# A fixed order on TensorE in the modulation loop, x loaded between weights, and one projection less ahead of a scan tree

## The chip, the cores and the metric

The kernel runs on one core of one Trainium2 chip. The metric is the device time of one execution in microseconds (us). Three timed executions of the kernel before gave 2169.12, 2169.86 and 2171.75 us. The changed kernel is timed in the same way.

The engines are named as the profile names them: PE is TensorE (matmuls), PEld its weight loads, DVE is VectorE, ACT is ScalarE, POOL is GpSimd, and SP is SyncE, which here only issues DMA transfers. Every engine works through its own list of instructions strictly in order; a waiting instruction holds up all that stand behind it.

## The reference

The reference is one layer of a hybrid network on 1024 latent tokens of width 1024, with 256 context tokens beside them. All data is fp32. What matters here is its beginning:

```python
m_lat = (jax.nn.silu(c) @ w_mod[l] + b_mod[l]).reshape(B_, 1, N_MOD, D)
m_ctx = (jax.nn.silu(c_ctx) @ w_mod[l] + b_mod[l]).reshape(N_MOD, D)
h_lat = rms_norm(x, norm_mix[l]) * (1.0 + m_lat[:, :, 1]) + m_lat[:, :, 0]
h_ctx = rms_norm(ctx, norm_mix[l]) * (1.0 + m_ctx[1]) + m_ctx[0]
... = features(h_lat, w_in[l], ...)        # one projection for three mixers and the gates
... = features(h_ctx, w_in[l], ...)
yc_ctx, s_f, s_b = hgrn2_bidir(ccq, ccf, ccb, cci, ccg, lbf[l], lbb[l], gn_c[l], s0, s0)
yc = hgrn2_bidir(cq, cf, cb, ci, cg, lbf[l], lbb[l], gn_c[l], s_f, s_b)[0]
```

So the modulation vectors come first, then the normed and modulated context and latents, then the projections of the context. A gated recurrence over the context gives a state per head and direction (`s_f`, `s_b`), and the same recurrence over the latents starts from it. Its forget gates use lower bounds `lbf`, `lbb`, which depend on two small inputs alone. Windowed and global attention, the merge of the branches and a gated MLP follow. The change leaves all of them as they are.

## The kernel before, in words

Tiles have 128 partitions; the width 1024 is cut into `KT` = 8 blocks. A large matmul is done in three products (high part by high part, high by low, low by high), for which ACT casts a weight tile to its high part (`w_unit`, L174) and DVE subtracts to get the low part (L175). The raw weights go through three rotating buffers each of the tags `wr`, `wh` and `wl`; the context's weights are used raw (`w_raw`, L186).

A scheduling layer sets the order of instructions on each engine. It takes the program's operations, their dependences, their place in the program and priorities (`tc.high_priority`), and decides which ready operation comes next on each engine; a pool hands out the buffers. The order is fixed when the program is built.

The stages that the change touches, in order of time:

- **The modulation loop** (L312 to L350). Eight weight tiles `wm0` to `wm7` of 1 MB are loaded by SP. For six of them PE multiplies by `silu(c)` (`pr`, L331), ACT copies the row out (L333), PE turns it (`pm`, L293) and DVE makes shift and scale of it (L284, L286). For blocks 1 and 4 (`MOD_OFF`) DVE does the product itself (`acc`, L322 and L325), and PE only turns the result (`pt`, L344). At `i == NORMAT` (3) `ctx_norm` makes the context's RMS: ACT squares, DVE sums (`css`, L300), PE turns (`rcc`, L237), DVE and POOL take the power -1/2 (L247, L248), and PE spreads the result over all partitions with two matmuls (`rpc`, L258). From then on `ctx_h` makes the modulated context block by block: DVE L306, ACT L308 (`ch`). The tiles `pr`, `pt` and `rpc` share two PSUM banks of tag "b".
- **The lower bounds** (L351 to L360): a load of 4 KB, six small DVE operations and one exponential on ACT, after the loop.
- **The context's projections, woven with the latents' norm** (`weave` at L458). `ctx_c` does for four heads the units f, b and v (`czf`, `czb`, `czv`), `ctx_kv` then keys and values (`ckv`). `lat_norm` loads x row-wise (`xn`, four buffers), squares and sums it on ACT (L380), then loads x turned, as eight tiles of 512 KB (`x32`, L384), spreads the RMS (`rpx`), and makes from each tile the high and low parts `hh` and `hl` of the normed latents with two DVE operations and one on ACT (`finish_h`, L263 to L265).
- **The early projections**: `zq` and `zf` of head 0 (48 matmuls of 512 columns each). Only two tiles of this kind (`mm2`) fit at once, so the third, `zb`, waits until `zq` has been read by ACT (L1037) and DVE (`qr`, L1038).
- **The context's recurrence.** DVE folds the keys in a tree of eight levels (L473, L476); for each head PE turns the result (`ckp`, L483), ACT copies it (`ckt`, L485), PE multiplies it with the values (`cu`, L489) and ACT copies the state out (`st_ctx`, L490). `ckt` has one buffer.
- **The recurrence over the latents** (`hgrn_head`), attention, merge and MLP, some 2000 us, follow.

Of the kernel before, what the change touches and what calls it, by code (L numbers as in the profile page):

```python
# [12 lines left out]
AF = mybir.ActivationFunctionType  # L13
ALU = mybir.AluOpType
# [4 lines left out]
P = 128  # L19
D = 1024  # L20
KT = D // P
L = 1024
LT = L // P
LC = 256
# [22 lines left out]
WAT = 5  # L47
MPRIO = 100
CXAT = 1
NORMAT = 3  # L50

MOD_OFF = (1, 4)
# [38 lines left out]
def build(tc, ins, out, dbg=None):  # L91
    nc = tc.nc
    V, A, G, T, SP = nc.vector, nc.scalar, nc.gpsimd, nc.tensor, nc.sync
    with ExitStack() as top:
# [46 lines left out]
        lbr = cs([P, 8], "lbr")  # L141
# [60 lines left out]
        def gemm_tm(psl, ws, h, toks, k0=0, nk=KT):  # L202

            hh, hl = h
            for k in range(nk):
# [3 lines left out]
                T.matmul(psl, hh[:, k, toks], wl[:, k % 4, :], start=False, stop=False)  # L209
                T.matmul(psl, hl[:, k, toks], wh[:, k % 4, :], start=False, stop=e)  # L210


        def rms_row(pool, parts, n, name, tag="b", on_pe=False):

            return rms_bc(rms_r(pool, parts, n, name, on_pe), n, name, tag)
# [45 lines left out]
        def finish_h(t, r, a, bi, ohh, ohl, x=None):  # L261

            V.scalar_tensor_tensor(out=t, in0=t if x is None else x, scalar=a, in1=r, op0=ALU.mult, op1=ALU.mult)  # L263
            A.activation(ohh, t, AF.Identity, bias=bi)
            V.scalar_tensor_tensor(out=ohl, in0=t, scalar=bi, in1=ohh.bitcast(F32), op0=ALU.add, op1=ALU.subtract)  # L265

        with ExitStack() as s0:
# [28 lines left out]
            def ctx_norm():  # L296
                csq = xm_.tile([P, KT, LC], F32, tag="csq", name="csq")
                A.activation(csq, cx, AF.Square)
                css = xm_.tile([P, LC], F32, tag="css", name="css")
                V.reduce_sum(out=css, in_=csq.rearrange("p k t -> p t k"), axis=AX.X)  # L300
                return rms_row(xm_, [css], LC, "c")

            def ctx_h():
                while pend:
# [2 lines left out]
                                           op0=ALU.mult, op1=ALU.mult)  # L307
                    A.activation(ch[:, k], cx[:, k], AF.Identity, bias=m01[:, k, 0, 1:2])  # L308

            for i in range(KT):  # L310
                wm = xm_.tile([P, 2, KT, P], F32, tag="wm", name=f"wm{i}", bufs=WM)
                SP.dma_start(wm, ins["w_mod01"][i].rearrange("p (j k c) -> p j k c", j=2, k=KT))  # L312
                if i == CXAT:
                    SP.dma_start(cx, ins["ctxT"].rearrange("(k p) t -> p k t", p=P))
                if WAT <= i < WAT + 3:
                    units0.append(w_raw(ins["w_cm"][U_C["fbv"[i - WAT]]], KT, P))
                if i in MOD_OFF:
                    acc = accs[i] = xm_.tile([P, 2, 2, P], F32, tag="acc", name=f"acc{i}", bufs=2)
                    for k in range(KT):
                        for v in range(2):  # L320
                            if k == 0:
                                V.tensor_scalar(out=acc[:, v], in0=wm[:, :, k], scalar1=scc[:, k, v:v + 1], scalar2=None,  # L322
                                                op0=ALU.mult)
                            else:
                                V.scalar_tensor_tensor(out=acc[:, v], in0=wm[:, :, k], scalar=scc[:, k, v:v + 1],  # L325
                                                       in1=acc[:, v], op0=ALU.mult, op1=ALU.add)
                    continue
                pr = bank("b", f"pr{i}", (P, 2, P))
                with tc.high_priority(offset=MPRIO):
                    for k in range(KT):  # L330
                        T.matmul(pr[0:2], scc[:, k], wm[:, :, k], start=k == 0, stop=k == KT - 1)  # L331
                    row = xm_.tile([2, 2, P], F32, tag="row", name=f"row{i}", bufs=3)
                    A.copy(row, pr[0:2])  # L333
                rows.append((i, row))
                if len(rows) > 1:
                    mod_row(*rows.pop(0))
                if i == KT - 1:
                    mod_row(*rows.pop(0))
                for n in MOD_FIN.get(i, ()):
                    pm = xm_.tile([P, 2, 2], F32, tag="pm", name=f"pm{n}")  # L340
                    pt = bank("b", f"pt{n}", (P, 2, 2, P))
                    for v in range(2):
                        for j in range(2):
                            T.transpose(pt[:, j, v], accs[n][:, v, j], ident)  # L344
                    V.reduce_sum(out=pm, in_=pt, axis=AX.X)
                    mod_done(n, pm)
                if i == NORMAT:
                    rc = ctx_norm()
                if i >= NORMAT:
                    ctx_h()  # L350
            SP.dma_start(lbr, ins["lb"])  # L351
            SP.dma_start(gnc, ins["gn"])

            V.tensor_tensor(out=lt, in0=lbr, in1=lbr, op=ALU.subtract)
            A.activation(lt, lt, AF.Exp)
            V.reciprocal(lb, lt)
            V.tensor_tensor(out=lt, in0=lt, in1=lb, op=ALU.mult)
            V.tensor_tensor(out=lt, in0=lt, in1=lt, op=ALU.subtract)
            V.tensor_scalar(out=lb, in0=lt, scalar1=0.0, scalar2=1.0, op0=ALU.max, op1=ALU.min)
            V.tensor_scalar(out=oml, in0=lb, scalar1=-1.0, scalar2=1.0, op0=ALU.mult, op1=ALU.add)  # L360
            xw.close()
            hpool = top.enter_context(ExitStack())
            hp = Aligned(hpool.enter_context(tc.tile_pool(name="hp", bufs=1, reuse_waits="tile")))
# [8 lines left out]
            def lat_norm():  # L372

                nt = L // P
                rl = xq.tile([P, nt], F32, tag="rs", name="rsx")
                for t in range(nt):
                    xn = xq.tile([P, D], F32, tag="xn", name=f"xn{t}", bufs=4)
                    SP.dma_start(xn, ins["x"][t * P:(t + 1) * P, :])
                    sq = xq.tile([P, D], F32, tag="sq", name=f"sqx{t}", bufs=2)
                    A.activation(sq, xn, AF.Square, accum_out=rl[:, t:t + 1])  # L380
                    if t % 2:
                        yield
                for k in range(KT):
                    SP.dma_start(x32[:, k], ins["xT"][k * P:(k + 1) * P, :])  # L384
                rp = rms_bc(rms_pow(rl), L, "x", "b")
                yield
                for k in range(KT):
                    finish_h(x32[:, k], rp, a01[:, k, 0:1], m01[:, k, 0, 0:1], hh[:, k], hl[:, k])
                    yield

            def proj(nm, h):

                w = w_unit(ins["w_cm"][U_C[nm] + h], KT, P)
                z = mm2(f"z{nm}{h}")
                for hf in range(2):
                    gemm_cm(z[:, hf], w, H, slice(hf * 512, hf * 512 + 512))
                return z.rearrange("p a b -> p (a b)")
# [1 line left out]

            knb = ct([P, 64], "knb")  # L400
            qnb = ct([P, 64], "qnb")
            A.dma_start(knb, ins["kn"].to_broadcast([P, 64]))
            A.dma_start(qnb, ins["qn"].to_broadcast([P, 64]))
            cp = Aligned(s0.enter_context(tc.tile_pool(name="cp", bufs=1, reuse_waits="tile")))
            cK = cp.tile([P, 2, CH, LC], F32, tag="cK", name="cK")
            cF = cp.tile([P, 2, CH, LC], F32, tag="cF", name="cF")
# [24 lines left out]

            def ctx_kv():

                for br in range(2):
                    ws = [w_raw(ins["w_tm"][(br * 3 + 2) * 2 + kh], 4, 256) for kh in range(2)]
                    for tt in range(2):
                        z = bank("b", f"ckv{br}{tt}", (P, 256))
                        for k in range(KT):
                            T.matmul(z, ch[:, k, tt * P:(tt + 1) * P], ws[k // 4][:, k % 4], start=k == 0,
                                     stop=k == KT - 1)  # L440
                        kv = cp.tile([P, 256], F32, tag="ckvs", name=f"ckvs{br}{tt}", bufs=2)
                        if br == 0:
# [15 lines left out]
            weave((ctx_all(), 14), (lat_norm(), 13))  # L458
            xin.close()

            early = {(nm, 0): proj(nm, 0) for nm in "qf"}
            cp2 = Aligned(s0.enter_context(tc.tile_pool(name="cp2", bufs=1, reuse_waits="tile")))

            Fp = cF
# [1072 lines left out]
```

## Time and profile before

| | us |
|---|---|
| three timed executions, lowest / median / highest | 2169.12 / 2169.86 / 2171.75 |
| the profiled execution's own time | 2173.9 |
| its span from first to last instruction | 2172.1 |
| PE busy | 2092.8 |
| DVE, ACT, POOL busy | 1434.3, 993.6, 396.1 |
| DMA, HBM read and written | 181.68 MB and 45.61 MB |

The profile is one execution, recorded by the hardware. A row of the timeline gives the start, the duration, the engine, the line, the operation and its tiles, and in brackets how long the engine sat idle just before and what ended that. The view of waits sums such idle time by what ended it. A table of windows gives for chosen stretches each engine's busy time, the clock that TensorE was granted (1.00 is full speed), the share of the DMA engines that was busy, and GB/s. A row of a group has the number of instructions behind the x, then busy us and mean ns. Durations of matmuls overlap: one record of 0.39 us follows another after 0.23 us.

### The profile page before, as it was taken

The numbers are of one execution on the slowest core, as the hardware profiler recorded it, in microseconds if no ns is written. First come the engines' busy times: TensorE is split into PE (matmuls) and PEld (weight loads), VectorE is DVE, ScalarE is ACT, GpSimd is POOL, SyncE is SP. The second block draws the span as 40 slices with busy tenths as digits, with TensorE's granted clock in tenths as the row PEclk, the third lists the DMA queues.
The fourth block names the chain that finished last, engine by engine and source line by source line (L and its number), as shares of the span: only waits on it lengthen the run. The fifth ranks groups of instructions, "written<-read, shape, count | busy, mean of one in ns | idle before, by whom it ended". The sixth has DMA issues, their size and how long they took to land. (4 is left out here: it accounts for less than half of the span.)

```text
span 2172.1 us, 30936 instructions
## 1 busy us (share of the span) xinstructions
PE 2092.8 (96%) x11610; PEld 1737.9 (80%) x11610; DVE 1434.3 (66%) x2578; ACT 993.6 (46%) x1800; POOL 396.1 (18%) x374
## 2 busy tenths in 40 slices
PE   7999999999999999999999999999899999999997
PEld 3878888789988788877777788887788888888887
DVE  4736666636566677679999856668877777764433
ACT  3323333311122777677777743445444444453322
POOL 0000000001022122123323300011434433200111
PEclk9999999999999999999999999999999999999999
DMA  8511110126653211221010254551222222286342
GB/s 323 219 46 31 49 46 29 53 82 195 197 163 116 92 54 45 71 66 30 30 35 27 69 198 159 179 169 61 93 77 84 87 79 88 79 276 199 106 129 91
DMA packets 95493, 229.30 MB, mean 106 GB/s; under 512 B 10736, under 2 KB 35824, under 8 KB 94320
## 3 DMA queue, kind: packets, MB, share of 16 engines
q1 hardware_dynamic: 95056, 227.26, 31.6%
q8 instruction: 91, 1.49, 0.3%
q14 instruction: 58, 0.48, 0.1%
q10 hardware_dynamic: 288, 0.07, 0.0%
HBM read 181.68 MB, written 45.61 MB: 105 GB/s over the span
## 5 line engine op out<-in xcount | busy, mean ns | idle before, releaser
L175 DVE TENSOR_TENSOR wl<-wr,wh 128x1024 fp32r<-128x1024 f32 x137 | 173.0, 1264 | 246.3 <-ACT wh L174 233.0
L174 ACT CAST wh<-wr 128x1024 fp32r<-128x1024 f32 x137 | 142.9, 1044 | 411.0 <-PE dn L903 71.7
L1279 DVE TENSOR_TENSOR pl<-pp,ph 128x512 fp32r<-128x512 f32 x236 | 159.0, 684 | 9.8 <-ACT ph L1278 8.5
L198 PE MATMUL gz<-hh,wh 128*128 128x512 f32 x384 | 156.3, 407 | 4.1 <-ACT gs L508 4.0
L1278 ACT CAST ph<-pp 128x512 fp32r<-128x512 f32 x236 | 136.3, 585 | 43.7 <-PE pp L1274 40.2
L200 PE MATMUL gz<-hh,wl 128*128 128x512 f32 x384 | 151.7, 395 | 0.0
L199 PE MATMUL gz<-hl,wh 128*128 128x512 f32 x384 | 151.6, 395 | 0.0
L209 PE MATMUL tm<-wl,hh 128*128 128x256 f32 x384 | 108.9, 284 | 2.7 <-DVE wl L175 2.7
L208 PE MATMUL tm<-wh,hh 128*128 128x256 f32 x384 | 108.8, 283 | 0.1
L210 PE MATMUL tm<-wh,hl 128*128 128x256 f32 x384 | 108.7, 283 | 0.0
L1269 PE MATMUL po<-pl,VHL 128*128 128x512 f32 x236 | 98.9, 419 | 7.6 <-DVE pl L1279 7.3
L1268 PE MATMUL po<-ph,VHL 128*128 128x512 f32 x236 | 104.8, 444 | 1.3 <-ACT ph L1278 1.3
L903 PE MATMUL dn<-ac,wh 128*128 128x512 f32 x256 | 99.7, 390 | 0.0
L904 PE MATMUL dn<-ac,wl 128*128 128x512 f32 x256 | 99.6, 389 | 0.0
L902 PE MATMUL dn<-ac,wh 128*128 128x512 f32 x256 | 99.6, 390 | 0.0
L1274 PEld LDWEIGHTS pp<-ident,plat 128*128 128x128 f32 x512 | 61.2, 140 | 34.3 <-DVE pl L1279 21.8
L1274 PE MATMUL pp<-ident,plat 128*128 128x128 f32 x512 | 78.2, 275 | 10.2 <-DVE pl L1279 9.9
L198 PEld LDWEIGHTS gz<-hh,wh 128*128 128x128 f32 x384 | 72.7, 189 | 18.4 <-ACT gs L508 6.2
L200 PEld LDWEIGHTS gz<-hh,wl 128*128 128x128 f32 x384 | 72.5, 189 | 15.3
L199 PEld LDWEIGHTS gz<-hl,wh 128*128 128x128 f32 x384 | 72.7, 189 | 11.6
L716 ACT ACTIVATE u<-c,cw 128x1024 f32<-128x1024 f32 x40 | 49.8, 1246 | 68.1 <-DVE c L863 37.1
L209 PEld LDWEIGHTS tm<-wl,hh 128*128 128x128 f32 x384 | 73.7, 192 | 3.7 <-DVE wl L175 3.4
(1478 smaller groups left out, 6094.5 us busy)
## 6 DMA issues: line engine op xcount, KB each, us to landing
wr<-in_w_cm SPq DMA_DIRECT2D x48, 512.0 KB, 3.7
wr<-in_w_up SPq DMA_DIRECT2D x44, 512.0 KB, 3.5
wr<-in_w_down SPq DMA_DIRECT2D x33, 512.0 KB, 3.7
wmr<-in_w_mod SPq DMA_DIRECT2D x32, 512.0 KB, 4.4
gate_d<-gs SPq DMA_DIRECT2D x48, 256.0 KB, 2.3
sgt<-gate_d SPq DMA_DIRECT2D x24, 512.0 KB, 3.3
act_d<-u SPq DMA_DIRECT2D x22, 512.0 KB, 2.6
st<-act_d SPq DMA_DIRECT2D x44, 256.0 KB, 4.5
```

The costliest lines, as they stand in the source:

```text
L174: A.copy(hi[:, :n], raw[:, :n])
L175: (lo_eng or V).tensor_tensor(out=lo[:, :n], in0=raw[:, :n], in1=hi[:, :n].bitcast(F32), op=ALU.subtract)
L198: T.matmul(psl, wh[:, k, c], hh[:, k0 + k, cols], start=s, stop=False)
L199: T.matmul(psl, wh[:, k, c], hl[:, k0 + k, cols], start=False, stop=False)
L200: T.matmul(psl, wl[:, k, c], hh[:, k0 + k, cols], start=False, stop=e)
L208: T.matmul(psl, hh[:, k, toks], wh[:, k % 4, :], start=s, stop=False)
L209: T.matmul(psl, hh[:, k, toks], wl[:, k % 4, :], start=False, stop=False)
L210: T.matmul(psl, hl[:, k, toks], wh[:, k % 4, :], start=False, stop=e)
L1268: T.matmul(po, vv, ph, start=n == 0, stop=False)
L1274: T.transpose(pp[:, h], PT(h, n), ident)
L1278: A.copy(ph, pp)
L1279: V.tensor_tensor(out=pl, in0=pp, in1=ph.bitcast(F32), op=ALU.subtract)
```

## The change

Five edits, all in the first part of the program:

1. The modulation loop is put into a section in which PE's instructions keep the order in which the code writes them. For that the code spreads the context's RMS (`rms_bc`, the matmuls `rpc`) at `i == NORMAT + 2` and no longer right after the norm, and `ctx_h` runs from there.
2. The lower bounds move from behind the loop into it, at `i == LBAT` (3).
3. Four of the eight tiles of turned x are loaded before the RMS is spread, and the other four one by one, each with a step of `finish_h`, so that they stand between the context's weights in SP's list.
4. Three small loads (`knb`, `qnb` from ACT's list, `gnc` from behind the loop) move into `ctx_kv` on SP.
5. Only `zq` is written ahead of the tree. `zf` comes from `hgrn_head`, so behind the tree and `cu` in the program.

```diff
+LBAT = 3
...
+        def lower_bounds():
+
+            SP.dma_start(lbr, ins["lb"])
+            V.tensor_tensor(out=lt, in0=lbr, in1=lbr, op=ALU.subtract)
+            A.activation(lt, lt, AF.Exp)
...
-                return rms_row(xm_, [css], LC, "c")
+                return rms_r(xm_, [css], LC, "c", False)
...
+            mo = ExitStack()
+            mo.enter_context(tc.manual_schedule(engines={mybir.EngineType.PE}))
             for i in range(KT):
...
+                if i == LBAT:
+                    lower_bounds()
...
                 if i == NORMAT:
                     rc = ctx_norm()
-                if i >= NORMAT:
+                if i == NORMAT + 2:
+                    rc = rms_bc(rc, LC, "c", "b")
+                if i >= NORMAT + 2:
                     ctx_h()
-            SP.dma_start(lbr, ins["lb"])
-            SP.dma_start(gnc, ins["gn"])
...
+            mo.close()
...
-                for k in range(KT):
-                    SP.dma_start(x32[:, k], ins["xT"][k * P:(k + 1) * P, :])
+                def x_load(k):
+                    if k < KT:
+                        SP.dma_start(x32[:, k], ins["xT"][k * P:(k + 1) * P, :])
+
+                for k in range(4):
+                    x_load(k)
                 rp = rms_bc(rms_pow(rl), L, "x", "b")
                 yield
                 for k in range(KT):
+                    x_load(k + 4)
                     finish_h(x32[:, k], rp, a01[:, k, 0:1], m01[:, k, 0, 0:1], hh[:, k], hl[:, k])
...
-            A.dma_start(knb, ins["kn"].to_broadcast([P, 64]))
-            A.dma_start(qnb, ins["qn"].to_broadcast([P, 64]))
...
+                SP.dma_start(knb, ins["kn"].to_broadcast([P, 64]))
+                SP.dma_start(qnb, ins["qn"].to_broadcast([P, 64]))
+                SP.dma_start(gnc, ins["gn"])
...
-            early = {(nm, 0): proj(nm, 0) for nm in "qf"}
+            early = {("q", 0): proj("q", 0)}
```

How this moves instructions is seen at three places. The first is PE's list in the modulation loop, from the turn of the context's sums (`rcc0`) to the first context unit (`czf0`). Before:

```order
L237 MATMUL rcc0_203<-ident_89,css_200 128x128 x2
L293 MATMUL pm3_252<-ident_89,row3_182 128x2 x2
L258 MATMUL rpc_209<-ident_89,rsc_202 128x128
L331 MATMUL pr5_241<-wm5_237,scc_83 2x256 x8
L258 MATMUL rpc_209<-ident_89,rsc_202 128x128
L293 MATMUL pm5_274<-ident_89,row5_250 128x2 x2
L331 MATMUL pr6_263<-wm6_259,scc_83 2x256 x8
L344 MATMUL pt4_280<-ident_89,acc4_220 128x128 x4
L293 MATMUL pm6_307<-ident_89,row6_272 128x2 x2
L331 MATMUL pr7_296<-wm7_292,scc_83 2x256 x8
L293 MATMUL pm7_312<-ident_89,row7_305 128x2 x2
L420 MATMUL czf0_350<-ch_111,wr1_239 128x256 x8
```

And the same place now:

```order
L249 MATMUL rcc0_213<-ident_89,css_210 128x128 x2
L347 MATMUL pr5_242<-wm5_238,scc_83 2x256 x8
L305 MATMUL pm3_253<-ident_89,row3_192 128x2 x2
L270 MATMUL rpc_258<-ident_89,rsc_212 128x128 x2
L347 MATMUL pr6_273<-wm6_269,scc_83 2x256 x8
L305 MATMUL pm5_284<-ident_89,row5_251 128x2 x2
L360 MATMUL pt4_290<-ident_89,acc4_221 128x128 x4
L347 MATMUL pr7_306<-wm7_302,scc_83 2x256 x8
L305 MATMUL pm6_317<-ident_89,row6_282 128x2 x2
L305 MATMUL pm7_322<-ident_89,row7_315 128x2 x2
L432 MATMUL czf0_350<-ch_111,wr1_240 128x256 x8
```

The product `pr5` has moved ahead of the two matmuls `rpc`, between which it stood, and `pm6` has moved behind `pr7`.

The second place is SP's list where the turned x (`x32`) is loaded; `wr7`, `wh8`, `wl9` are the context's weights f, b, v of the third head, and the next three those of the fourth. Before:

```order
L186 DMA wl6_480<-in_w_cm 128x1024
L384 DMA x32_116<-in_xT 128x1024 x8
L186 DMA wr7_503<-in_w_cm 128x1024
L186 DMA wh8_522<-in_w_cm 128x1024
L186 DMA wl9_541<-in_w_cm 128x1024
L186 DMA wr10_564<-in_w_cm 128x1024
```

Now:

```order
L394 DMA x32_116<-in_xT 128x1024 x4
L187 DMA wr7_500<-in_w_cm 128x1024
L187 DMA wh8_520<-in_w_cm 128x1024
L394 DMA x32_116<-in_xT 128x1024
L187 DMA wl9_540<-in_w_cm 128x1024
L394 DMA x32_116<-in_xT 128x1024
L187 DMA wr10_564<-in_w_cm 128x1024
L394 DMA x32_116<-in_xT 128x1024
```

Four loads of x, not eight, now stand ahead of `wr7`; the rest alternate with the weights.

The third place is PE's list around the context's recurrence, between the early projections and `zb`. Before, behind all 48 matmuls of `zf0`:

```order
L200 MATMUL zf0_762<-hh_334,wl18_759 128x512
L483 MATMUL ckp0_844<-ident_89,cK_347 128x128 x4
L483 MATMUL ckp1_859<-ident_89,cK_347 128x128 x4
L489 MATMUL cu00_851<-cV_349,ckt0_849 128x128 x2
L489 MATMUL cu01_855<-cV_349,ckt0_849 128x128 x2
L483 MATMUL ckp2_874<-ident_89,cK_347 128x128 x4
L489 MATMUL cu10_866<-cV_349,ckt1_864 128x128 x2
L489 MATMUL cu11_870<-cV_349,ckt1_864 128x128 x2
L483 MATMUL ckp3_889<-ident_89,cK_347 128x128 x4
```

Now, behind all of `zq0`:

```order
L201 MATMUL zq0_710<-hh_336,wl17_707 128x512
L498 MATMUL ckp0_792<-ident_89,cK_347 128x128 x4
L498 MATMUL ckp1_807<-ident_89,cK_347 128x128 x4
L199 MATMUL zf0_872<-hh_336,wh18_868 128x512
L200 MATMUL zf0_872<-hl_337,wh18_868 128x512
L504 MATMUL cu00_799<-cV_349,ckt0_797 128x128 x2
L504 MATMUL cu01_803<-cV_349,ckt0_797 128x128 x2
L498 MATMUL ckp2_822<-ident_89,cK_347 128x128 x4
L201 MATMUL zf0_872<-hh_336,wl18_869 128x512
L199 MATMUL zf0_872<-hh_336,wh18_868 128x512
L504 MATMUL cu10_814<-cV_349,ckt1_812 128x128 x2
L504 MATMUL cu11_818<-cV_349,ckt1_812 128x128 x2
```

The recurrence's small matmuls have moved from behind `zf0` into its beginning, two to four matmuls of `zf0` between one head's and the next. Behind `zb0` PE's list is the same as before.

More of the change, by code (lines that the diff above doesn't have):

```diff
@@ L210, in gemm_tm @@
                 T.matmul(psl, hl[:, k, toks], wh[:, k % 4, :], start=False, stop=e)
+        def lower_bounds():
+            SP.dma_start(lbr, ins["lb"])
+            V.tensor_tensor(out=lt, in0=lbr, in1=lbr, op=ALU.subtract)
+            A.activation(lt, lt, AF.Exp)
+            V.reciprocal(lb, lt)
+            V.tensor_tensor(out=lt, in0=lt, in1=lb, op=ALU.mult)
+            V.tensor_tensor(out=lt, in0=lt, in1=lt, op=ALU.subtract)
+            V.tensor_scalar(out=lb, in0=lt, scalar1=0.0, scalar2=1.0, op0=ALU.max, op1=ALU.min)
+            V.tensor_scalar(out=oml, in0=lb, scalar1=-1.0, scalar2=1.0, op0=ALU.mult, op1=ALU.add)
         def rms_row(pool, parts, n, name, tag="b", on_pe=False):
@@ L348, in build @@
                     rc = ctx_norm()
-                if i >= NORMAT:
+                if i == NORMAT + 2:
+                    rc = rms_bc(rc, LC, "c", "b")
+                if i >= NORMAT + 2:
                     ctx_h()
-            SP.dma_start(lbr, ins["lb"])
-            SP.dma_start(gnc, ins["gn"])
[L354 to L360, printed above, removed]
+            mo.close()
             xw.close()
```

## The prediction

> **What bounds the kernel now.** I read the page's first lines, then a table of four stages, then PE's waits in the first three of them, then the places where these waits stand.
>
> ```profile
> span 2172.1 us, 30936 instructions
> PE 2092.8 (96%) x11610; PEld 1737.9 (80%) x11610; DVE 1434.3 (66%) x2578; ACT 993.6 (46%) x1800; POOL 396.1 (18%) x374
> ...
> core 0: us, PE busy (x) PEld busy (x) DVE busy (x) ACT busy (x) POOL busy (x), PEclk, DMA share, GB/s
> 0.00:42.96 42.96, 29.08 (x120) 11.12 (x121) 23.06 (x67) 11.50 (x22) 1.36 (x6) 0.96 0.86 334
> 42.96:103.94 60.98, 58.43 (x330) 52.83 (x329) 40.99 (x62) 28.33 (x50) 2.54 (x2) 0.97 0.64 237
> 103.94:150.76 46.82, 42.11 (x195) 34.57 (x193) 10.43 (x16) 9.68 (x21) 0.87 (x2) 0.93 0.18 55
> 150.76:2172.10 2021.34, 1963.15 (x10971) 1639.39 (x10969) 1359.79 (x2433) 944.12 (x1709) 391.29 (x365) 1.00 0.30 98
> ```
>
> PE is busy 96% of the span, and from 150.76 us on, where its order is unchanged, 97% at full clock. So what PE gains before 150.76 should move all the rest forward, and the question is how much it gains in three stages: the modulation loop (to 42.96), the context's projections (to 103.94), and `zq`, `zf`, the context's recurrence and `zb` (to 150.76). PE's waits there:
>
> ```profile
> PE pr L331 <- DMA wm<-in_w_mod: 8.8, 2, 7.7
> PE czf L420 <- DMA wr<-in_w_cm: 2.6, 1, 2.6
> PE zb L198 <- DVE qr L1038: 2.5, 1, 2.5
> PE rpc L258 <- POOL rsc L248: 2.3, 1, 2.3
> PE cu L489 <- ACT ckt L485: 2.2, 4, 0.8
> ```
>
> The 8.8 us are the first loads, which the change doesn't touch. Behind three of the others (`czf`, `zb`, `rpc`) the clock drops, which costs nearly as much again:
>
> ```profile
> 25.00:30.00 5.00, 3.74 (x10) 1.25 (x11) 4.58 (x14) 0.00 (x0) 0.88 (x1) 0.66 1.01 413
> ...
> 65.07:67.60 2.53, 0.00 (x0) 0.02 (x1) 2.53 (x3) 1.44 (x3) 0.00 (x0) 1.00 1.02 409
> 67.60:72.80 5.20, 5.18 (x16) 4.35 (x17) 5.20 (x6) 2.59 (x3) 0.00 (x0) 0.67 1.03 410
> ...
> 125.80:137.20 11.40, 6.69 (x51) 5.50 (x49) 2.96 (x5) 7.36 (x16) 0.00 (x0) 0.94 0.22 65
> 137.20:142.49 5.29, 5.29 (x13) 4.13 (x14) 3.06 (x3) 0.52 (x1) 0.00 (x0) 0.50 0.00 0
> ...
> 150.76:161.64 10.88, 10.88 (x50) 9.01 (x48) 9.62 (x14) 4.00 (x6) 0.00 (x0) 1.00 0.15 48
> ```
>
> **Part A, the modulation loop.** The timeline of PE:
>
> ```profile
> 23.40 0.38 PE L237 MATMUL rcc<-ident,css 128*128 128x128 f32 x2
> ...
> 26.26 0.32 PE L258 MATMUL rpc<-ident,rsc 128*128 128x128 f32 x1 [2.27 <-POOL rsc L248]
> ...
> 26.51 5.30 PE L331 MATMUL pr<-wm,scc 128*2 128x256 f32 x16
> ...
> 31.74 0.32 PE L258 MATMUL rpc<-ident,rsc 128*128 128x128 f32 x1
> ...
> 32.53 3.62 PE L331 MATMUL pr<-wm,scc 128*2 128x256 f32 x16
> ...
> 38.09 3.62 PE L331 MATMUL pr<-wm,scc 128*2 128x256 f32 x16 [0.57 <-DVE pm L345]
> ...
> 42.75 0.28 PE L293 MATMUL pm<-ident,row 2*128 2x2 f32 x2 [1.04 <-ACT row L333]
> 42.96 3.72 PE L420 MATMUL czf<-ch,wr 128*128 128x256 f32 x16
> ```
>
> PE waits 2.27 us for POOL with the first `rpc`, while `pr5` stands behind it; then the second `rpc` stands behind `pr5`, so DVE's first product with it starts only at 32.1. Now `pr5` fills the wait. From the end of `rcc` (23.8, or 24.1, since `pm0` now stands behind `pr2` and takes its 0.3 here) I add: `pr5` 3.45 at full clock to 27.55; `pm3` 0.3; `rpc`, whose input comes at about 28.0 as DVE has 1.5 us of lower bounds ahead of it, to 28.4; `pr6` 3.45; `pm5` 0.3; then, as in the rows between 32.53 and 42.96, a wait of 0.5, `pt4` 0.66, a wait of 0.6, `pr7` 3.45, `pm6` 0.28, a wait of 0.5 and `pm7` 0.28. That ends at 38.5 in place of 42.96. The weights don't set it:
>
> ```profile
> 13.19 0.33 SPq L312 DMA_DIRECT2D wm<-in_w_mod  x1
> ...
> DMA to landing us min/median/max: 5.0/13.8/18.1
> ```
>
> That is the last issue of `wm7`, and the longest time to landing of all eight: it is there by 31.3, and `pr7` starts at 34.0 in my sum. The unknown is the lower bounds. DVE now waits for their load in the middle of the loop, and the norm's sums stand behind it.
>
> ```profile
> lbr<-in_lb SPq DMA_DIRECT2D x1, 4.0 KB, 14.0
> ```
>
> Issued at about 6 us, right behind `wm3`, it lands between 18 (`wm3`'s landing, as transfers end nearly in their order here) and 20; DVE is busy with the context's sum to 20.0. So 0 to 1 us is lost, and ACT's exponential may hold up a row by 0.5. I take 4.2 us for A, between 2 and 5.
>
> **Part B, the context's projections.** PE stands still for 2.53 us at 65.07 because `wr7` is late, and then does `czf` in 5.20 us at a clock of 0.67, where a unit otherwise follows after 3.45. That is 2.53 + 1.75 = 4.3 us. Why it is late:
>
> ```profile
> 42.47 6.41 SPq L378 DMA_DIRECT2D xn<-in_x  x4
> ...
> 49.41 4.60 SPq L384 DMA_DIRECT2D x<-in_xT  x8
> 55.74 0.33 SPq L186 DMA_DIRECT2D wr<-in_w_cm  x1
> 57.01 0.33 SPq L186 DMA_DIRECT2D wh<-in_w_cm  x1
> ```
>
> It stands behind eight loads of 512 KB. At 410 GB/s one takes 1.28 us, which is also the distance of the last two issues. Four fewer ahead bring it 5.1 us earlier, at about 62.5. But PE also asks earlier, by the 4.2 us of A. What feeds the x loads comes earlier too: SP issued the fifth `xn` at 42.47 only when ACT had squared the first, behind the modulation's rows, and ACT now gets there some 3 to 4 us sooner. So `wr7` lands at about 59 and is needed at 61.8. The loads behind it alternate, 2.56 us for a weight and an x, against 3.45 of PE for a unit. The last x tiles come later, and DVE makes `hl` of them:
>
> ```profile
> 79.23 2.47 DVE L265 SCALAR_TENSOR_TENSOR hl<-x,m,hh 128x1024 fp32r<-128x1024 f32 x2
> ```
>
> That chain ended at 81.7 and was not needed before 103.94. It now ends at about 80 and is needed at 95.7, so it is hidden; were it not, `zq` would wait for the last `hl`. I take B as 4.3, less 0.3 for `rpx`, since one square now stands behind a head's sigmoids: 4.0, between 0 and 4.3. The three small loads add SP issues of 0.3 to 0.4 us each, beside PE.
>
> **Part C, the recurrence beside `zf`.** Between 125.94 and 137.20 PE does only the small matmuls:
>
> ```profile
> L489 PE MATMUL cu<-cV,ckt 128*128 128x128 f32 x32 | 4.6, 288 | 2.2 <-ACT ckt L485 2.2
> ...
> L485 ACT COPY ckt<-ckp 128x512 f32<-128x512 f32 x4 | 2.4, 588 | 0.0
> L483 PE MATMUL ckp<-ident,cK 128*128 128x128 f32 x16 | 2.2, 272 | 0.0
> L490 ACT COPY st_ctx<-cu 128x128 f32<-128x128 f32 x8 | 2.1, 266 | 3.9 <-PE cu L489 3.9
> ```
>
> It idles 2.2 us for `ckt` and 2.5 us for `qr`: ACT reaches the sigmoid of `zq` only behind the last `st_ctx`. Then `zb` runs at a clock of 0.50. From 137.20 to 150.76 it takes 13.56 us where the next projection takes 10.88, a loss of 2.7. Together 7.4 us. Now matmuls of `zf` stand between the heads. One head takes ACT and PE in turn about 2.0 us (two copies of state, one of `ckt`, and `cu`), and PE now has 1.16 of `cu`, 0.5 of `ckp` and 0.46 of two matmuls of `zf`, together 2.1. So the turn is covered. And some 8 us of `zf` remain behind the last head, in which ACT and DVE need 2.3 us to free `zq`'s banks: `zb` starts without a wait. What is left is the first `cu`, about 0.5 us, since ACT casts a weight (1.05) ahead of the first `ckt`. I take 6.9, between 4 and 7.4. DVE's tree has to be done when `zq` ends:
>
> ```profile
> 104.36 0.68 DVE L473 TENSOR_TENSOR cK<-cK,cF 128x512 f32<-128x512 f32 x1
> ```
>
> The tree ended at 105.0, and `zq` at 115.1. Two more low parts (1.23 each) now stand within it, but it starts with the context's last unit, 8 us earlier: about 99, against 106.6.
>
> **The sum.** 4.2 + 4.0 + 6.9 = 15.1 us off the profiled execution's 2173.9 gives 2158.8. That execution lies 4.0 above the median of the timed ones, 2169.86, so the forecast is 2154.8, say 2155 us. With each part at its low end the gain is 6 us (2164), at its high end 16.7 (2153).
>
> A measurement of this kernel can't tell less than about 0.2% (4.3 us) from no change.
>
> **The rivals.**
>
> *One part does not come.* Either `wr7` shares the DMA engines with what is issued behind it and is late all the same, or the lower bounds or a row on ACT hold the loop back. For it: the DMA engines are busy all through this stretch (share 1.02 at 409 GB/s). Against: `wr7` has 2.8 us of room. Price about 4 us: 2159. Chance 0.12.
>
> *The cold clock was chance.* If the stretches at 0.66, 0.67 and 0.50 were not in the timed executions, the change takes only idle time away, and 1.75 + 2.7 + 1.8 (the `pr5` of 5.30) of my sum go: 15.1 - 6.3 = 8.8, so 2161. Against: the three times lie within 2.6 us. Chance 0.06. The Trainium skill has a rule for it in "TensorE: Matmul & The Clock Gate", in the section on the clock gate: TensorE runs at half rate after an idle window of about 3.4 us, and the window runs freely, so how many matmuls are slow varies between runs. The trace agrees with the half rate (0.50), but drops after idle times of 2.3 to 2.5 us.
>
> *The tree ends too late.* The low parts within it wait for weights of which the second waits for a free buffer; if that adds more than 7 us, `ckp` waits, and now all of `zf` behind it on PE. Part C is then lost: 2162. For it: DVE works strictly in order. Against: the 7 us of room. Chance 0.05.
>
> *Weights late all through, slower.* The later weights use other buffers in turn than before. If that lets loads start later, PE waits for a load, a cast and a low part: 3.5 + 1.05 + 1.23 = 5.8 us each time. From four exposed units on the gain is gone and more: 2155 + 23 = 2178. For it: the raw weights have three buffers for some 135 units. Against: PE's waits for weights are now 2.7 us where they are longest, and SP's list has one load of weights more, not fewer, ahead at this point:
>
> ```profile
> L209 PE MATMUL tm<-wl,hh 128*128 128x256 f32 x384 | 108.9, 284 | 2.7 <-DVE wl L175 2.7
> ```
>
> Chance 0.04.
>
> *Nothing to see.* The gain is taken back by a wait behind 150.76, where DVE or ACT sets the pace: 2169. PE's 97% there speak against it. Chance 0.05.
>
> **How the numbers follow.** The forecast has 0.68. Faster by over 0.2%, so under 2165.5: 0.68 + 0.12 + 0.06 + 0.05 = 0.91. Within 0.2%: 0.05. Slower: 0.04. The range goes from 2150, three below the sum of the high ends as the timed executions spread by 2.6, to 2163, which takes in the first three rivals.
>
> **What would show it.** The first `czf` near 38.5 and not 42.96; no wait for `wr` at the third head and a clock of 1.00 there; `zq` from about 95.7; `cu` waits under 1 us, no wait of `zb` for `qr`, and `zb` from about 124.6 at full clock; from there to the end 2021 + 10.9 us as before. It is wrong if a wait for DMA or DVE appears before `zq`, or if the stretch behind `zb` has become longer.

## The result: 2155.2 us, 0.7% faster

The changed kernel takes 2155.16 us (median of six executions, 2154.72 to 2157.16), the kernel before in the same comparison 2170.40 us (six, 2169.12 to 2174.56). The ratio is 0.993, with a 95% interval of 0.9919 to 0.9942. The forecast was 2155, with a range of 2150 to 2163.

The page of the changed kernel, and the table of the four stages, cut at the same instructions as before (first `czf`, first `zq`, first `zv`), with two short windows behind them: the third head's `czf`, and `zb`.

```profile
span 2152.9 us, 30935 instructions
PE 2084.3 (97%) x11610; PEld 1732.2 (80%) x11610; DVE 1434.3 (67%) x2578; ACT 993.4 (46%) x1800; POOL 394.5 (18%) x374
```

```profile
0.00:38.04 38.04, 26.23 (x120) 10.43 (x121) 22.76 (x67) 11.16 (x21) 1.36 (x6) 1.00 0.93 367
38.04:95.03 56.99, 56.73 (x330) 51.45 (x329) 41.98 (x65) 28.82 (x51) 1.79 (x2) 1.00 0.68 255
95.03:134.25 39.22, 39.17 (x195) 32.16 (x194) 9.68 (x15) 9.79 (x21) 2.15 (x2) 1.00 0.23 74
134.25:2152.90 2018.65, 1962.18 (x10971) 1638.19 (x10969) 1359.89 (x2433) 943.64 (x1709) 389.17 (x365) 1.00 0.30 98
60.45:64.10 3.65, 3.65 (x19) 3.23 (x18) 3.65 (x4) 1.72 (x3) 0.00 (x0) 1.00 1.03 412
123.36:134.25 10.89, 10.89 (x50) 9.01 (x49) 4.34 (x4) 2.90 (x4) 0.00 (x0) 1.00 0.14 48
```

Behind the first loads PE stands still for 0.3 us in the second stage and not at all in the third, and the granted clock is 1.00 throughout, at the third head and in `zb` too. (The column has 1.00 for the first product `pr0` as well, which takes 5.27 us where the later ones take 3.62; no run here shows why.) The stages gave 42.96 - 38.04 = 4.9 us, 60.98 - 56.99 = 4.0 and 46.82 - 39.22 = 7.6, together 16.5. The last stage is 2.7 us shorter with the same instructions; the last section comes back to that. So the two profiled executions differ by 19.2 us, the medians by 15.2: the profiled execution of before lies 3.5 above its median, that of after is the fastest of its six.

PE's waits in the first 150 us, complete:

```profile
PE pr L347 <- DMA wm<-in_w_mod: 10.4, 2, 7.7
PE pr L347 <- DVE pm L361: 0.8, 1, 0.8
PE pt L360 <- ACT row L349: 0.3, 1, 0.3
PE pm L305 <- ACT row L349: 0.3, 1, 0.3
PE rpx L270 <- POOL rsx L260: 0.3, 1, 0.3
```

Of the five waits shown of before only the first is left. It is 10.4 in place of 8.8: the first product `pr0` took 5.27 us and not 6.18, and `pm0`, with a wait of 0.45 of its own before, now stands behind `pr2`; `pr2` starts at 15.7 in both.

### The profile page after: what moved, and what is told of

It reads as the page before. It is cut to its first block, busy times and chain, and to the rows that moved or that the text cites. A ratio compares the mean times of both kernels' runs of the same rounds, so it can differ in the third digit from the quotient of the medians.

```text
span 2152.9 us, 30935 instructions
## 1 busy us (share of the span) xinstructions
PE 2084.3 (97%) x11610; PEld 1732.2 (80%) x11610; DVE 1434.3 (67%) x2578; ACT 993.4 (46%) x1800; POOL 394.5 (18%) x374
## 5 line engine op out<-in xcount | busy, mean ns | idle before, releaser
L201 PEld LDWEIGHTS gz<-hh,wl 128*128 128x128 f32 x384 | 72.2, 188 | 15.2
```

Of the source, the lines that this page charges most:

```text
L201: T.matmul(psl, wl[:, k, c], hh[:, k0 + k, cols], start=False, stop=e)
```

## The experiments

A is the modulation loop, B the order of the loads of x, C `zf` behind the tree. The labels: e1 to e4 each undo one thing in the changed kernel, e8 undoes all of A, e5 and e6 put C alone and B alone into the kernel before, e7 fills a wait, f1 and f2 go on from the changed kernel. Ratios are to the kernel before, run beside each; its medians were 2169.72 to 2171.0.

| kernel | first `czf` | to `zq` | to `zv` | rest | median us | ratio (95%) |
|---|---|---|---|---|---|---|
| before | 42.96 | 60.98 | 46.82 | 2021.34 | 2170.40 | 1 |
| the change | 38.04 | 56.99 | 39.22 | 2018.65 | 2155.16 | 0.9919 to 0.9942 |
| the change again | 37.99 | 56.99 | 39.21 | 2020.31 | 2153.78 | 0.9911 to 0.9938 |
| e1, C undone | 37.79 | 57.00 | 45.67 | 2016.94 | 2161.89 | 0.9953 to 0.9978 |
| e2, B undone | 38.21 | 59.30 | 39.22 | 2018.17 | 2156.75 | 0.9933 to 0.9960 |
| e8, A undone | 42.42 | 56.53 | 39.20 | 2015.05 | 2159.35 | 0.9933 to 0.9956 |
| e5, C alone | 43.05 | 59.29 | 39.20 | 2024.96 | 2163.79 | 0.9954 to 0.9978 |
| e6, B alone | 42.82 | 57.00 | 47.17 | 2016.01 | 2165.59 | 0.9970 to 0.9987 |
| e3, A without rpc's place and order | 40.77 | 57.00 | 39.21 | 2018.32 | 2157.12 | 0.9928 to 0.9953 |
| e3b, A without fixed order | 39.12 | 57.00 | 39.21 | 2018.07 | 2154.88 | 0.9914 to 0.9939 |
| e4, bounds late | 39.86 | 57.00 | 39.21 | 2014.23 | 2154.97 | 0.9925 to 0.9950 |
| e7, e1 with filler | 39.96 | 56.99 | 45.23 | 2017.02 | 2161.24 | 0.9943 to 0.9967 |
| f1, `rpc` in another bank | 36.30 | 57.41 | 39.20 | 2016.69 | 2154.44 | 0.9907 to 0.9934 |
| f2, f1 with filler | 37.38 | 57.41 | 39.21 | 2017.10 | 2152.39 | 0.9899 to 0.9926 |

The four columns of stages come from one profiled execution each, the medians from 4 to 11.

**e1: C undone.**

```diff
-            early = {("q", 0): proj("q", 0)}
+            early = {(nm, 0): proj(nm, 0) for nm in "qf"}
```

> The changed kernel with zf written ahead of the tree again (part C undone). In the profiles, from the start of zq to the end of zb the stage took 46.8 us before and 39.0 after, a difference of 7.8. Theory (idle time and the cold clock behind it come back together): 2155.2 + 7.8 = 2163, with waits of PE for ckt near 2.2 us and for qr near 2.5, and a granted clock near 0.5 at the beginning of zb. Rival (the cold clock was chance): only the idle time comes back, 4.7 us, so 2160. Rival (the tree, not zf, set this stage): no difference, 2155.

PE's waits from `zq` to `zv`, and windows of the recurrence (117.00 to 128.09) and of `zb` (its first 5.3 us, then all of it):

```profile
PE zb L199 <- DVE qr L1053: 2.5, 1, 2.5
PE cu L504 <- ACT ckt L500: 2.2, 4, 0.8
```

```profile
117.00:128.09 11.09, 6.33 (x49) 5.24 (x47) 2.96 (x5) 7.16 (x16) 0.00 (x0) 0.98 0.20 66
128.09:133.40 5.31, 5.31 (x17) 4.33 (x18) 3.06 (x3) 0.52 (x1) 0.00 (x0) 0.72 0.00 0
128.09:140.46 12.37, 12.37 (x48) 10.15 (x49) 3.06 (x3) 0.55 (x2) 0.00 (x0) 0.88 0.00 0
```

Both waits are back at their old size, and `zb` is slow again, though by 12.37 - 10.89 = 1.5 us and not by 2.7. The stage costs 6.5 us, the median 6.7, the ratio 7.8 (0.9966 against 0.9930). This is C: the median, 2161.89, lies between the two theories (2163 with the clock, 2160 without), and it loses as much as the stage does.

**e2: B undone.**

```diff
-                for k in range(4):
+                for k in range(KT):
                     x_load(k)
                 for k in range(KT):
-                    x_load(k + 4)
```

> The changed kernel with all eight tiles of turned x loaded ahead of the context's weights (part B undone). The first x tile goes out at 44.2 us after the change and went out at 49.4 before; with eight of them ahead, wr7 then lands near 67.5 - 5.2 = 62.3, and PE wants it at 60.45. Theory: a wait of about 1.9 us for wr7, and 0 to 1.8 for the clock behind it: 2157 to 2159. Rival (wr7 shares the DMA engines with what is issued behind it, so its place does not matter): no new wait, 2155. Rival (PE asks earlier, the loads do not come earlier): a wait of 7 us, 2164.

Rows of PE's waits, of its timeline and of SP's:

```profile
PE czf L431 <- DMA wr<-in_w_cm: 1.3, 1, 1.3
PE czf L431 <- ACT cF L1022: 0.9, 1, 0.9
```

```profile
61.64 3.69 PE L431 MATMUL czf<-ch,wr 128*128 128x256 f32 x16 [1.33 <-DMA wr<-in_w_cm]
```

```profile
44.87 4.80 SPq L394 DMA_DIRECT2D x<-in_xT  x8
50.61 0.33 SPq L187 DMA_DIRECT2D wr<-in_w_cm  x1
```

The wait for `wr7` comes back at half its size, 1.3 us, and with it 0.9 us for ACT, a head later; the `czf` behind the wait for `wr7` is at full clock (3.69, where before had 5.20). So here B is worth 2.3 us in the profile, and not 4; by time it is 1.6 in the medians and 3.5 by the ratios, with intervals that overlap the change's. The loop moves both sides: `wr7` is issued at 50.61 and no longer at 55.74, 5.1 us earlier, and needed 4.8 us earlier. So the loop by itself takes little from the wait; it is shorter than in before mostly because the load landed 10.9 us after its issue and not 11.7. That this time differs without the loop too, e5 below shows: there the loop and the order of the loads are those of before, and the load took 11.2.

**e5 and e6: C alone and B alone in the kernel before.**

```diff
-            early = {(nm, 0): proj(nm, 0) for nm in "qf"}
+            early = {("q", 0): proj("q", 0)}
```

> The kernel before with only part C (zf behind the tree). Theory (the parts add up): 2170.4 - 7.8 = 2162.6. Rival (the tree ends too late, as the loop and the context are later too): PE waits for the tree, and the gain is under 4, 2166.

```diff
-                for k in range(KT):
-                    SP.dma_start(x32[:, k], ins["xT"][k * P:(k + 1) * P, :])
...
+                for k in range(4):
+                    x_load(k)
...
                 for k in range(KT):
+                    x_load(k + 4)
```

> The kernel before with only part B (four tiles of turned x ahead of the weights, four between them). Theory: the wait of 2.5 us for wr7 and the cold clock behind it (1.75) go: 2170.4 - 4.2 = 2166.2. Rival (only the idle time goes, the cold clock is chance): 2168.

C alone gives a ratio of 0.9966, 7.4 us (4.8 to 10.0), and the third stage of the change (39.20). B alone gives 0.9979, 4.6 us (2.8 to 6.5), and the second stage of the change (57.00). Both medians (2163.79 and 2165.59) lie nearer to the theory on record than to its rival. Rows of e5 at the two waits that it keeps, and two of its waits:

```profile
28.03 0.32 PE L258 MATMUL rpc<-ident,rsc 128*128 128x128 f32 x1 [2.27 <-POOL rsc L248]
28.28 3.62 PE L331 MATMUL pr<-wm,scc 128*2 128x256 f32 x16
```

```profile
66.94 3.69 PE L420 MATMUL czf<-ch,wr 128*128 128x256 f32 x16 [1.79 <-DMA wr<-in_w_cm]
```

```profile
PE czf L420 <- DMA wr<-in_w_cm: 1.8, 1, 1.8
PE czf L420 <- ACT cF L1008: 0.5, 1, 0.5
```

In the kernel before the same 2.27 us for `rpc` were followed by a `pr5` of 5.30 us; here it takes 3.62. The loop ends no earlier for it (43.05): here `pr2` was slow, 8.76 us for `pr2` and `pr3` together where before had 7.07. And the second stage is 59.29, within 0.01 of e2's 59.30, though e2 has the changed loop and e5 the old one. In both the `czf` behind the wait is at full clock, and both wait 2.3 us in all for `wr7` and ACT. So B removes about 2.3 us of idle time whatever the loop is, and the other 1.7 of its 4.0 came with the slow `czf` of the one profile of before.

Windows of e6, the recurrence and then `zb`:

```profile
121.66:133.07 11.41, 6.70 (x51) 5.51 (x49) 2.96 (x5) 7.36 (x16) 0.00 (x0) 0.97 0.21 65
133.07:138.36 5.29, 5.29 (x13) 4.14 (x14) 3.06 (x3) 0.52 (x1) 0.00 (x0) 0.50 0.00 0
133.07:146.99 13.92, 13.92 (x49) 11.21 (x49) 3.06 (x3) 0.55 (x2) 0.00 (x0) 0.78 0.00 0
```

That is a loss of 13.92 - 10.89 = 3.0 us. So the wait for `qr` is the same 2.5 us in before, e1 and e6, and what the clock adds behind it is not the same.

**e8: all of A undone.** It takes the diffs of e3 and e4 below together.

> The changed kernel with the whole of part A undone: no fixed order, the RMS spread right behind the norm, the lower bounds behind the loop. PE's order in the loop is that of the kernel before, with the second rpc behind pr5. Theory (parts add up): the first context unit starts at 43.0 and not at 38.0, 2155.2 + 4.9 = 2160.1. Rival (a late start of the context is made up, since the loads set its end): 2157 or less.

The first `czf` starts at 42.42, the median is 2159.35, near the theory (43.0 and 2160.1). Against the two medians of the change, A is worth 4.2 to 5.6 us; by the ratios (0.9945 against 0.9930 and 0.9924) 3.3 to 4.6, with intervals that overlap a little. The profiles differ by 42.42 - 38.04 = 4.4, of which a `pr5` of 4.82 us in place of 3.62 is 1.2. What is left in e8 is B, C and the three small loads of the fourth edit, which have no run of their own: B alone and C alone add to 12.0 us by the ratios, e8 has 11.9, so no price of the small loads shows.

**e3, e3b and e4: the pieces of A.** e3 leaves out the fixed order and spreads the RMS at `NORMAT` again; e3b leaves out the fixed order alone (the first removed line of this diff); e4 leaves the lower bounds behind the loop.

```diff
-            mo.enter_context(tc.manual_schedule(engines={mybir.EngineType.PE}))
...
-                return rms_r(xm_, [css], LC, "c", False)
+                return rms_row(xm_, [css], LC, "c")
...
-                if i == NORMAT + 2:
-                    rc = rms_bc(rc, LC, "c", "b")
-                if i >= NORMAT + 2:
+                if i >= NORMAT:
                     ctx_h()
```

> The changed kernel without the fixed order and with the context's RMS spread right behind the norm, as before; the lower bounds stay early. PE then does both rpc ahead of pr5, so it waits for POOL, but rpc is no longer split around pr5. Theory (the wait for POOL and the cold clock behind it are what the order saves): a wait of 2 to 2.7 us and a pr5 of 5.3 instead of 3.6, 2155.2 + 4.4 = 2159.6. Rival (what cost was the second rpc standing behind pr5, which held DVE back): DVE starts on the context at about 27, and the loop ends within 1 us of the changed kernel's 38.0, 2156.

> The changed kernel without the section of fixed order, but with the RMS still spread two steps later. The scheduler then puts pr5 ahead of rpc by itself; only pm and pt stand in another order. Theory (what counts is that pr5 fills the wait for POOL, not the fixed order as such): the first context unit within 0.5 us of 38.0 (or of 39.8 with a slow second product), 2155. Rival (the fixed order saves by itself): 1 us or more later.

```diff
-                if i == LBAT:
-                    lower_bounds()
...
             mo.close()
+            lower_bounds()
```

> The changed kernel with the lower bounds behind the loop again; PE's order is unchanged. Theory (the early bounds neither cost nor gain: DVE gives 1.4 us for them where PE does not wait): 2155 within 1 us. Rival (behind the loop, the load of the exponential's table, 1.28 us, and the exponential stand ahead of the first square of x and the last row on ACT, so the first context unit and the x loads start about 1.5 us later): 2156.5.

The loop of e3, and behind it that of e3b:

```profile
26.18 0.43 PE L270 MATMUL rpc<-ident,rsc 128*128 128x128 f32 x2 [2.27 <-POOL rsc L260]
26.55 3.62 PE L346 MATMUL pr<-wm,scc 128*2 128x256 f32 x16
...
40.77 3.72 PE L429 MATMUL czf<-ch,wr 128*128 128x256 f32 x16
```

```profile
27.50 0.43 PE L270 MATMUL rpc<-ident,rsc 128*128 128x128 f32 x2
...
33.35 0.65 PE L359 MATMUL pt<-ident,acc 128*128 128x128 f32 x4 [1.45 <-ACT row L348]
...
39.12 3.72 PE L431 MATMUL czf<-ch,wr 128*128 128x256 f32 x16
```

In e3 the wait of 2.27 us came back, with both `rpc` ahead of `pr5` as expected, but I missed the clock: `pr5` behind the wait took 3.62 us and not 5.3. The median is 2157.12, where the record had 2159.6; the rival's loop, within 1 us of 38.0, did not come either. In e3b the scheduling layer puts `pr5` ahead of `rpc` by itself, once the code asks for `rpc` two blocks later: the wait is gone without a fixed order. So in the profiles the place of `rpc` gives 1.65 us (40.77 to 39.12), and the fixed order another 1.1 (39.12 to 38.04, mostly that `pt4` waits 1.45 and not 0.3). By time neither is shown: the intervals of e3, e3b and the change overlap, and the medians of e3b and the change in the same comparison are 2154.88 and 2153.78.

In e4 the loop ends at 39.86, but 1.7 of the 1.8 us more than the change stand in one product, this row of its timeline, which takes 3.62 us in the change:

```profile
15.70 5.30 PE L345 MATMUL pr<-wm,scc 128*2 128x256 f32 x16 [2.06 <-DMA wm<-in_w_mod]
```

PE's list is the same as the change's there. Without that product the two loops end within 0.2 us, and the median of 2154.97 lies with the change. So the early bounds bring nothing and cost nothing that these runs can see. DVE's first operation on them in the change, which has no wait in brackets:

```profile
19.76 0.15 DVE L216 TENSOR_TENSOR lbs<-lbr 128x8 f32<-128x8 f32 x1
```

**e7: is the slow `zb` a matter of the idle time before it?** e1, with 14 small matmuls behind the last `cu`, whose result nobody reads.

```diff
+            dm = bank("a", "dm", (P, 512))
+            for n in range(14):
+                T.matmul(dm[:, 0:P], st_ctx[:, 3, 1], ident, start=True, stop=True)
```

> The kernel with part C undone (zf ahead of the tree), and 14 matmuls of 128 columns whose result nobody reads, put behind the last cu, where PE would wait for qr; they need the last state, so they fill about 2.0 of the 2.5 us and end before qr. They add work and take no wait away. Theory (the slow beginning of zb is the clock, which drops because PE stood still): zb runs at full clock, 2.7 us less than with part C undone alone: about 2160. Rival (zb is slow for another reason, for instance what DVE and ACT do beside it): the same as with part C undone alone, about 2163.

The filler and then `zb`:

```profile
128.05:131.20 3.15, 3.15 (x29) 3.15 (x29) 2.25 (x3) 2.71 (x3) 0.00 (x0) 1.00 0.00 0
131.20:142.18 10.98, 10.98 (x52) 9.10 (x51) 2.10 (x2) 0.03 (x1) 0.00 (x0) 1.00 0.00 0
```

`zb` takes 10.98 us at full clock, where without filler it took 12.37, 13.56 and 13.92 behind the same 2.5 us of idle time. The filler runs some 0.9 us too long, so the stage is only 0.4 shorter than e1's, and the medians (2161.24 and 2161.89) don't differ by more than the executions spread. For the clock one profile speaks, in the expected direction; ACT and DVE also had less to do beside this `zb` (0.03 and 2.10 us, in e1 0.55 and 3.06), so that rival is not wholly out.

**The change again, f1 and f2.** The change run again has the expected stages within 0.05 us, and a median of 2153.78. f1 puts `rpc` into a bank that is idle then, since `pr`, `pt` and `rpc` share two; f2 also fills the wait for `wm2` with 12 small matmuls on `ident` whose result nobody reads.

> The changed kernel once more, unchanged, beside the next three. Theory (between executions only the clock at short waits differs): 2155 within 1.5 us; the stages lie as before except where a wait is followed by a cold clock: the first context unit at 38.0, or at 39.8 if the second product of the loop is slow; from there to zq 57.0, from zq to the end of zb 39.2; the rest between 2014 and 2025, as in the ten profiles so far. Rival (the first profile of the changed kernel was lucky within the three stages): one of the two later stages longer by over 1 us.

```diff
-            if n > 512:
+            if n > 512 or tag == "mm":
                 rp = mm2(f"rp{name}").rearrange("p a b -> p (a b)")
...
-                    rc = rms_bc(rc, LC, "c", "b")
+                    rc = rms_bc(rc, LC, "c", "mm")
```

> A further step on the changed kernel: rpc takes one of the large tiles' banks, which are idle then, so that pr, pt and czf need not share one bank while rpc holds the other. Theory: the waits of 0.8 (pr7 for DVE's reading of pt4) and of 0.3 go, and the first context unit starts 1.0 to 1.4 us earlier, 36.8 or 38.5 with a slow second product; 2154, which a comparison of times will hardly tell from the changed kernel. Rival (the loads of the third head's weights then come too late): PE waits for wr7, and zq starts no earlier.

```diff
+                if i == 2:
+                    dm = bank("a", "dm", (P, 512))
+                    for n in range(12):
+                        T.matmul(dm[:, 0:P], ident, ident, start=True, stop=True)
```

> The same as f1_bank, with 12 matmuls of 128 columns whose result nobody reads between the first and the second product of the loop, where PE waits 2.0 to 2.8 us for wm2; they fill about 1.7 us of it. Theory (a short idle time is what lets the clock drop there, now and then): the second product takes 3.6 us, never 5.3, and the mean over executions is 0.5 us less than without; in the profile the first context unit at 36.8. Rival (the clock drops there because PE had begun too late before): a product of 5.3 us all the same in some profile.

The loop of f1:

```profile
31.96 0.66 PE L360 MATMUL pt<-ident,acc 128*128 128x128 f32 x4
32.54 3.62 PE L347 MATMUL pr<-wm,scc 128*2 128x256 f32 x16
36.09 0.28 PE L305 MATMUL pm<-ident,row 2*128 2x2 f32 x2
36.30 1.56 PE L432 MATMUL czf<-ch,wr 128*128 128x256 f32 x6
```

The last three waits of the loop (0.3, 0.8 and 0.3 us) are gone. The last `pm` now stands within the first `czf`, at 37.79, so `zq` starts not 1.7 but 1.3 us earlier than in the change, at 93.71. In f2 `pr2` took 3.62 us, as expected, but the filler ran past the load: `pr2` starts at 16.48 and not at 15.76, and the first `czf` at 37.38, not at the 36.8 on record. By time neither f1 (2154.44) nor f2 (2152.39) is told from the change: its two medians are 2155.16 and 2153.78, and the intervals overlap. f2 has the lowest median of all; that it is faster than the change is not shown.

## Why the prediction was right, step by step

**The bound.** That PE's gains early on move all the rest forward held. The longest wait for a weight's low part further on (the second row), which stood for a shortage of weights, is 2.7 us as before, and the largest of the waits there (the first row) was 9.9 before. Other rows moved by up to 0.8 us either way; in all PE stands still for 2018.65 - 1962.18 = 56.5 us behind `zv`, where it was 58.2:

```profile
PE pp L1289 <- DVE pl L1294: 9.8, 20, 0.8
...
PE tm L210 <- DVE wl L176: 2.7, 2, 1.4
```

So the rivals that took the gain back later, slower or nothing to see, fell.

**Part A, forecast 4.2 us, measured 4.9 in the profiles.** The first `czf` came at 38.04, 0.5 ahead of the forecast; part of that is that the row's and DVE's waits left in the loop sum to 1.4 and not 1.6. The lower bounds, put at 0 to 1 us on DVE and 0.5 on ACT, cost nothing. The cause I gave, `pr5` filling the wait for POOL, is shown by the profiles of e3 and e3b: with `rpc` ahead the wait is there, with `pr5` ahead it is not. But 1.7 of the 4.9 are `pr5` at full clock: 3.2 us are idle time and order, and e8 gives the same 3.2 (4.4 less 1.2).

**Part B, forecast 4.0, measured 4.0 in the profiles.** The SP rows of the change show the new order:

```profile
44.22 2.35 SPq L394 DMA_DIRECT2D x<-in_xT  x4
46.62 0.91 SPq L187 DMA_DIRECT2D wr<-in_w_cm  x1
```

`wr7` is issued at 46.62, 9.1 us earlier than before. By e2's 50.61 that is 5.1 from the loop, for which I had 3 to 4, and 4.0 from the four loads, for which I had 5.1. It landed 8.9 us later, at 55.5, where I had 59, and PE asks for it at 60.45 and doesn't wait. The 61.8 that I wrote for this does not follow from the terms beside it: 65.07 - 4.2 is 60.9, so the room was 1.9 us by my own sum, and it came out as 4.9. The 0.3 for `rpx` is there as forecast. The last `hl`, forecast for 80, is done at 78.4, 16.6 us ahead of `zq`:

```profile
75.88 2.48 DVE L277 SCALAR_TENSOR_TENSOR hl<-x,m,hh 128x1024 fp32r<-128x1024 f32 x2
...
94.04 0.68 DVE L488 TENSOR_TENSOR cK<-cK,cF 128x512 f32<-128x512 f32 x1
```

What I did not see is how much of the 4.0 was the clock of one profile: with the `czf` behind the wait at full clock the stage without B takes 59.3 us beside either loop (e2, e5), so that B removes 2.3 us of idle time, and 1.7 came with the profiled execution of before. That the forecast met 4.0 is in that part luck.

**Part C, forecast 6.9, measured 7.6 in the profiles.** The second of these rows is the tree's last fold. It ends at 94.7, where I forecast 99 and the need is at 106.2, so the rival of a late tree was further off than I gave it. PE at the recurrence:

```profile
106.16 1.03 PE L498 MATMUL ckp<-ident,cK 128*128 128x128 f32 x8
106.95 0.48 PE L199 MATMUL zf<-hh,wh 128*128 128x512 f32 x1
107.26 0.40 PE L200 MATMUL zf<-hl,wh 128*128 128x512 f32 x1
107.71 1.16 PE L504 MATMUL cu<-cV,ckt 128*128 128x128 f32 x8
```

The 0.5 us that I had kept for the first `cu` behind ACT's cast did not come, and that is most of what C gave more; `zb` starts at 123.36 in place of 124.6 because `zq` started 0.7 earlier and `cu` did not wait. e1, e5 and e8 show that the mechanism is this one edit: with it the stage takes 39.2 us whatever else is there, without it 45.2 to 47.2.

**The sum, 15.1 against 16.5 in the profiles and 15.2 in the medians.** The forecast met the medians better than its own terms deserve. The profiled execution of before had its cold stretches at their full 6.1 us (1.7 + 1.75 + 2.7), and I counted them as always there. The rival that they were chance I gave 0.06; it is in part true of two of the three. `pr5` behind the wait for `rpc` was slow in before, e6 and e8 (5.30, 5.30, 4.82) and not in e3 and e5 (3.62), though in e5 `pr2` had lost the same 1.7 us ahead of it; `czf` behind the wait for `wr7` was slow in before, not in e2 and e5; `zb` was slow in each of the three executions that have the wait (before, e1, e6), by 2.7, 1.5 and 3.0. So idle time alone gives 3.2 + 2.3 + 4.9 = 10.4 us, and the clock adds about 1.5 to 6 from one execution to the next. That the terms came out 1.4 too small and the typical execution loses less to the clock than the profiled one work against each other; the median can't divide them. By the ratios the single parts, 7.4 (C alone), 4.6 (B alone) and 3.3 to 4.6 (A, by e8; A alone was not run), add to 15.3 to 16.6, so nothing is lost between the parts that these runs can see.

## What to carry to other kernels

When one engine is busy nearly all the time, list its idle stretches in the part where it is not, and ask of each which ready work stands behind the waiting instruction: here a projection written behind the chain it used to precede was worth 0.3% of the time (C alone), and a small operation moved two blocks later took away a wait of 2.3 us in the profile. Price the idle time and the clock behind it as two terms, and give the second a chance of its own, from more than one profile: in one profile they look like one. When what a part brings alone (B: 4.0 us in its profile) is not what its removal costs (2.3), look for that second term first, before putting the difference down to another part: the other part can be tested by itself, as e5 does here.

## What the runs showed of the hardware

**The granted clock behind a short wait differs between executions of the same list of instructions.** Beside the three places above there is the wait for `wm2` at 15.7 us. `pr2` behind it was slow in e4, e5 and e7 and at full clock in the other ten profiles without filler there. The length of the wait does not decide it: in e7 2.10 us were followed by a slow product, in the change 2.75 us by a fast one, on the same list; first e7's row, then that of the change:

```profile
15.95 5.30 PE L347 MATMUL pr<-wm,scc 128*2 128x256 f32 x16 [2.10 <-DMA wm<-in_w_mod]
```

```profile
15.71 3.62 PE L347 MATMUL pr<-wm,scc 128*2 128x256 f32 x16 [2.75 <-DMA wm<-in_w_mod]
```

Where PE had been busy for only 6.3 to 6.7 of the 11.1 to 11.4 us before (the recurrence without `zf`), the clock fell in three of three. The Trainium skill, "TensorE: Matmul & The Clock Gate", in the section on the clock gate, says that activity is watched in a free-running window of about 3.4 us, so that the number of slow matmuls varies between runs. The variation agrees with these profiles; its idle window of 3.4 us is longer than any of the waits here that were followed by a slow stretch (1.25 to 2.55 us). No run here measures the window.

**The unchanged rest of the kernel is not a constant.** From `zv` to the end it took 2014.2 to 2025.0 us in the fourteen profiles, a spread wider than any part of the change is worth. Stretches at a clock of 0.5 to 0.85 appear there about 360, 470, 1380 and 1400 us behind `zv` in some executions and not in others (in f1 also at 785). Summed over windows of 4 us up to the end (one minus the clock, times the window's length), they and the slow end of each execution cost 5.7 to 10.2 us. Taken out, the rest still spreads from 2008.5 to 2014.7; what makes that spread stays open. So the 2.7 us that the last stage was shorter in the first pair of profiles are no effect of the change that these runs can show.
